# An encoder trunk's FFN: the second projection by seven block products, in three parts of the hidden columns

## The chip, the cores and the metric

The kernel runs on one core of one Trainium2 chip, as one program. Five engines each work through an instruction queue of their own, in order: TensorE (PE; its weight loads are shown as PEld), VectorE (DVE), ScalarE (ACT), GpSimd (POOL) and SyncE (SP, which here issues DMA transfers). They wait for each other by semaphores. Matmuls write into PSUM, of which this kernel has eight banks of 128 x 512 float32. The metric is the device time of one execution in microseconds.

## The reference

A trunk of two layers over 512 tokens of width 1024, all in float32. A layer has a SwiGLU FFN, a mixer (dilated window attention and a convolution branch) and a second FFN. Only the FFNs change:

```python
def swiglu_ffn(h, w_up, w_down):
    a, b = jnp.split(h @ w_up, 2, axis=-1)
    return (jax.nn.silu(a) * b) @ w_down

for l in range(DEPTH):
    x = x + 0.5 * swiglu_ffn(rmsnorm(x, ffn1_norm[l]), ffn1_w_up[l], ffn1_w_down[l])
    x = x + mixer(rmsnorm(x, mix_norm[l]), ...)
    x = x + 0.5 * swiglu_ffn(rmsnorm(x, ffn2_norm[l]), ffn2_w_up[l], ffn2_w_down[l])
    x = rmsnorm(x, final_norm[l])
```

`w_up` is 1024 x 5632, `w_down` 2816 x 1024. So there are four FFNs, each with a hidden width of 2816.

## The kernel before

Activations lie transposed in SBUF: a tile holds 128 features (the partitions) by 512 tokens. The residual x is eight such tiles, `xs[0]` to `xs[7]`. To keep float32 accuracy every operand is split into two parts in a rounded format (float32r): hi, a rounded copy that ScalarE makes, and lo, what is left, which VectorE makes by a subtraction (`split_to`, `stage`). A product is then three matmuls into the same PSUM bank, hi x hi, hi x lo and lo x hi (`mm3`, L157 to L159). The weights are the stationary operand, 128 x 128, and the 512 tokens stream past.

Weights come from DRAM in pieces of up to 1024 columns. `stage` (L151 to L153) transfers one into `raw` (two buffers, issued by SyncE), ScalarE makes `hi` and VectorE `lo` (four buffers each). `proj_cols` walks over such pieces for one or two output tiles.

An FFN has two halves. In the first, for each pair of the 22 hidden tiles, 96 matmuls compute the a and b columns into two banks each (`ps_a` from the three banks of tag `mm`, `ps_b` from the four of tag `at`); VectorE multiplies a by the norm's factors R (L248), ScalarE applies silu (L249), VectorE multiplies by b (L250), and the result is split into a hidden hi and lo tile. All 22 hidden tiles stay in SBUF (44 buffers of tag `h`). The second half, the second projection, goes over the output tiles in groups (0,1), (2,3), (4,5), 6, 7. A group sums over all 22 hidden tiles in its banks (`ps_d`), then VectorE multiplies by 0.5 R (L259) and adds to x (L260), and `after` prepares what the next block needs: the tile times the next norm's gain, split (`xgh`, L174; `xgl`, L175), and a running sum of squares (`sq`, L184 on ScalarE, L188 on VectorE).

Nobody wrote the order of the instructions by hand. A scheduler places each instruction on its engine's queue from the program's order, priorities (`tc.high_priority` moves weight pieces forward) and its own estimates of times; the queues are then fixed, and each engine runs its queue in order. A tile buffer is reused in a ring: who writes into it next waits until its last reader is done.

## Time and profile before

| | us |
|---|---|
| three runs | 2667.84, 2670.09, 2670.85; median 2670.09 |
| the profiled execution | 2669.43, of which its span 2667.5 |
| TensorE busy in the span | 2617.8 (98%), 12125 matmuls |
| VectorE / ScalarE busy | 1599.7 (60%) / 1005.8 (38%) |
| the four second projections | 119.68, 119.68, 119.68, 119.81 |

The span runs from the first instruction to the last. The profile names a group of instructions by line, engine, operation and tiles, as out<-in; `128x512` is partitions by elements. Matmul durations overlap in the pipeline, so the pace of a stage is its length over its matmuls, not the mean duration. "Idle before" is the time that an engine stood still ahead of an instruction, with the engine and tile that released it.

### The profile page before, as it was taken

How to read it: one execution, taken by the hardware profiler on the slowest of the kernel's cores; microseconds unless marked ns; L12 is line 12 of the kernel's file. 1: busy time of each engine (PE TensorE's matmuls, PEld its weight loads, DVE VectorE, ACT ScalarE, POOL GpSimd, SP SyncE). 2: the span in 40 equal slices, each digit the busy share in tenths (PEclk: the TensorE clock that was granted, in tenths of full speed). 3: DMA queues.
4: the chain of work that ended last, by engine and by line, in shares of the span. 5: the costliest groups of instructions: out<-in, count | busy, mean ns of one | idle time of the engine just before them, and what ended most of it. 6: DMA issues, size and time to landing. Idle time of an engine off the chain costs nothing.

```text
span 2667.5 us, 30985 instructions
## 1 busy us (share of the span) xinstructions
PE 2617.8 (98%) x12125; PEld 2125.9 (80%) x12125; DVE 1599.7 (60%) x2606; ACT 1005.8 (38%) x1572; POOL 110.5 (4%) x208
## 2 busy tenths in 40 slices
PE   8999999998999999999999999999989999999998
PEld 6888888776877788888888888887767778888887
DVE  4444349999985754443454433599999756444432
ACT  5332232233578242232332322322344963322222
POOL 1000000011011000000000000000011110000000
PEclk9999999999999999999999999999989999999999
DMA  4332333233333333332333322323323343333322
GB/s 155 98 95 91 103 99 105 79 113 97 100 112 110 117 95 96 102 95 95 95 95 95 100 94 93 108 91 114 96 85 121 100 126 103 95 95 96 102 91 75
DMA packets 253778, 268.65 MB, mean 101 GB/s; under 512 B 11624, under 2 KB 238320, under 8 KB 253632
## 3 DMA queue, kind: packets, MB, share of 16 engines
q1 hardware_dynamic: 242112, 234.91, 28.3%
q0 software_dynamic: 11504, 31.76, 4.0%
q8 instruction: 95, 1.56, 0.2%
q14 instruction: 51, 0.42, 0.1%
q10 hardware_dynamic: 16, 0.00, 0.0%
HBM read 251.75 MB, written 14.88 MB: 100 GB/s over the span
## 4 chain that ended last, share of the span: by engine, by line
PE 88%; DVE 7%; ACT 3%; issue 1%; DMA 0%; SPq 0%; ACTq 0%
PE ps_a L158 6%; PE ps_a L159 6%; PE ps_b L157 6%; PE ps_d L157 6%; PE ps_b L158 6%; PE ps_b L159 6%; PE ps_d L159 6%; PE ps_d L158 6%; PE ps_a L157 6%; PE ps_n L158 4%; PE ps_n L157 4%; PE ps_n L159 3%; DVE cv L516 2%; PE ps_cp L158 1%; PE ps_cp L159 1%; PE ps_cp L157 1%
## 5 line engine op out<-in xcount | busy, mean ns | idle before, releaser
L153 DVE TENSOR_TENSOR lo<-raw,hi 128x1024 fp32r<-128x1024 f32 (+1 forms) x448 | 539.2, 1204 | 725.0 <-ACT hi L152 724.0
L152 ACT ACTIVATE hi<-raw 128x1024 fp32r<-128x1024 f32 (+1 forms) x448 | 468.1, 1045 | 1058.3 <-issue 360.2
L516 DVE SCALAR_TENSOR_TENSOR cv<-u,cwc,cv 128x500 f32<-128x500 f32 (+14 forms) x480 | 335.7, 737 | 0.1
L158 PE MATMUL ps_b<-xgl,hi 128*128 128x512 f32 x704 | 275.1, 391 | 0.0
L157 PE MATMUL ps_a<-xgh,hi 128*128 128x512 f32 x704 | 273.5, 389 | 1.1 <-ACT xgh L174 1.1
L159 PE MATMUL ps_a<-xgh,lo 128*128 128x512 f32 x704 | 274.5, 390 | 0.0
L158 PE MATMUL ps_a<-xgl,hi 128*128 128x512 f32 x704 | 274.3, 390 | 0.1
L157 PE MATMUL ps_b<-xgh,hi 128*128 128x512 f32 x704 | 274.0, 389 | 0.0
L159 PE MATMUL ps_b<-xgh,lo 128*128 128x512 f32 x704 | 273.9, 389 | 0.0
L159 PE MATMUL ps_d<-sh,lo 128*128 128x512 f32 x704 | 273.9, 389 | 0.0
L157 PE MATMUL ps_d<-sh,hi 128*128 128x512 f32 x704 | 273.9, 389 | 0.0
L158 PE MATMUL ps_d<-sl,hi 128*128 128x512 f32 x704 | 273.9, 389 | 0.0
L158 PE MATMUL ps_n<-lo,xgh 128*128 128x512 f32 x576 | 228.7, 397 | 3.9 <-DVE lo L153 3.8
L159 PE MATMUL ps_n<-hi,xgl 128*128 128x512 f32 x576 | 225.7, 392 | 0.0
L157 PE MATMUL ps_n<-hi,xgh 128*128 128x512 f32 x576 | 215.8, 395 | 4.7 <-DVE tmp L379 3.4
L157 PEld LDWEIGHTS ps_a<-xgh,hi 128*128 128x128 f32 x704 | 132.0, 188 | 29.0 <-ACT xgh L174 1.5
L158 PEld LDWEIGHTS ps_b<-xgl,hi 128*128 128x128 f32 x704 | 132.2, 188 | 28.0 <-issue 0.7
L159 PEld LDWEIGHTS ps_b<-xgh,lo 128*128 128x128 f32 x704 | 132.2, 188 | 28.0 <-issue 0.7
L158 PEld LDWEIGHTS ps_a<-xgl,hi 128*128 128x128 f32 x704 | 132.2, 188 | 27.9 <-DVE xgl L175 0.5
L159 PEld LDWEIGHTS ps_d<-sh,lo 128*128 128x128 f32 x704 | 132.2, 188 | 27.5
L159 PEld LDWEIGHTS ps_a<-xgh,lo 128*128 128x128 f32 x704 | 132.2, 188 | 27.5 <-issue 0.2
L157 PEld LDWEIGHTS ps_b<-xgh,hi 128*128 128x128 f32 x704 | 132.2, 188 | 27.4
(234 smaller groups left out, 3988.1 us busy)
## 6 DMA issues: line engine op xcount, KB each, us to landing
raw<-in_ffn_w_up_dram SPq DMA_DIRECT2D x176, 512.0 KB, 3.5
raw<-in_w_in_dram SPq DMA_DIRECT2D x88, 512.0 KB, 3.6
raw<-in_ffn_w_down_dram SPq DMA_DIRECT2D x76, 512.0 KB, 3.5
raw<-in_w_in_dram SPq DMA_DIRECT2D x96, 256.0 KB, 3.1
raw<-in_w_conv_proj_dram SPq DMA_DIRECT2D x16, 512.0 KB, 3.5
raw<-in_w_out_dram SPq DMA_DIRECT2D x16, 512.0 KB, 3.5
vd<-tmp POOLq DMA_DIRECT2D x24, 256.0 KB, 2.3
od<-ot POOLq DMA_DIRECT2D x24, 256.0 KB, 3.0
```

Source lines behind the costliest of these rows:

```text
L152: nc.scalar.activation(hi[:, :m], raw[:, :m], AF.Copy)
L153: nc.vector.tensor_sub(lo[:, :m], raw[:, :m], hi[:, :m].bitcast(F32))
L157: nc.tensor.matmul(ps, ah, bh, start=first, stop=False)
L158: nc.tensor.matmul(ps, ah, bl, start=False, stop=False)
L159: nc.tensor.matmul(ps, al, bh, start=False, stop=last)
L516: nc.vector.scalar_tensor_tensor(a[:, t0:t1], u[k][:, t0 + d:t1 + d], cw(l, j, k), a[:, t0:t1], op0=ALU.mult, op1=ALU.add)
```

## The change

The second projection is computed by the seven-product scheme for 2 x 2 blocks. One block product has two hidden tiles (256 rows of `w_down`), two output tiles, and the tokens in two halves of 256. Directly that is 2 x 2 x 2 = 8 products of 128 x 128 weights by 256 tokens; here it is 7, of which four use sums of weight blocks and four use sums of hidden blocks. `stage7` transfers a weight piece (four hidden tiles by two output tiles), has VectorE form four sums (L251 to L253, tile `sm`) and splits both the raw piece and the sums into hi and lo (`split_to`, L166 and L167). `sums7` does the same for a pair of hidden tiles (tile `ts`, split into `Th` and `Tl`). `proj7` runs the seven products, each three matmuls of 256 columns, into four banks, two products side by side in three of them: the four `at` banks in even groups, the three `mm` banks and the `st` bank in odd ones. When a group is complete, ScalarE copies the first bank (`s1`, L298) and VectorE recombines the banks (L299 to L302, tile `o7`).

The FFN runs in three parts of 8, 8 and 6 hidden tiles: the first projection for these, then the second projection from these alone, added to x (`take`, L338 and L339; the second output tile of a pair comes out with the opposite sign). Hidden tiles and their sums have room for one part. In the last part, output tiles 6 and 7 are computed directly, and `after` runs there only. In all pairs of hidden tiles but the first, the b columns come before the a columns.

The queues change with it. On VectorE, in the second projection of the first FFN (`t<-ps_d` and `x` are the additions into x, `lo` a weight piece); waits name the engine waited for, and DMAHW a transfer. Before:

```order
L153 TENSOR_TENSOR lo_350_2300<-raw_348_2298,hi_349_2299 128x1024 [waits DMAHW1_49,PE_49,Activation_49]
L153 TENSOR_TENSOR lo_353_2330<-raw_351_2328,hi_352_2329 128x512 [waits DMAHW2_49,PE_49,Activation_49]
L153 TENSOR_TENSOR lo_365_2369<-raw_363_2367,hi_364_2368 128x1024 [waits DMAHW3_49,PE_49,Activation_49]
L153 TENSOR_TENSOR lo_368_2399<-raw_366_2397,hi_367_2398 128x1024 [waits DMAHW4_49,PE_49,Activation_49]
L153 TENSOR_TENSOR lo_371_2429<-raw_369_2427,hi_370_2428 128x768 [waits DMAHW5_49,PE_49,Activation_49]
L259 SCALAR_TENSOR_TENSOR t_354_2346<-ps_d_334_2176,R_34_240 128x512 [waits PE_49]
L260 TENSOR_TENSOR x4_85<-x4_85,t_354_2346 128x512 [waits DVE_49]
L259 SCALAR_TENSOR_TENSOR t_358_2356<-ps_d_335_2177,R_34_240 128x512 [waits PE_49]
L153 TENSOR_TENSOR lo_379_2464<-raw_377_2462,hi_378_2463 128x1024 [waits DMAHW6_49,Activation_49]
L260 TENSOR_TENSOR x5_86<-x5_86,t_358_2356 128x512 [waits DVE_49]
```

Now, at the end of the first part's second projection:

```order
L338 SCALAR_TENSOR_TENSOR t_163_1084<-o7_160_1074,R_34_240 128x512
L299 TENSOR_TENSOR o7_180_1203<-ps_7_165_1088,s1_181_1204 128x2x256 [waits PE_49]
L252 TENSOR_TENSOR sm_195_1277<-sm_195_1277,raw_194_1276 128x256 [waits DVE_49]
L339 TENSOR_TENSOR x2_83<-x2_83,t_162_1081 128x512 [waits DVE_49]
L167 TENSOR_TENSOR lo_197_1283<-raw_194_1276,hi_196_1282 128x1024 [waits PE_49,Activation_49]
L339 TENSOR_TENSOR x3_84<-x3_84,t_163_1084 128x512 [waits DVE_49]
L300 TENSOR_TENSOR o7_180_1203<-ps_7_166_1089,o7_180_1203 128x512 [waits DVE_49]
L253 TENSOR_TENSOR sm_195_1277<-sm_195_1277,raw_194_1276 128x256 [waits DVE_49]
L301 TENSOR_TENSOR o7_180_1203<-ps_7_166_1089,o7_180_1203 128x256 [waits DVE_49]
L302 TENSOR_TENSOR o7_180_1203<-ps_7_167_1090,o7_180_1203 128x512 [waits DVE_49,PE_49]
L338 SCALAR_TENSOR_TENSOR t_182_1210<-o7_180_1203,R_34_240 128x512 [waits DVE_49]
L167 TENSOR_TENSOR lo_199_1287<-sm_195_1277,hi_198_1286 128x1024 [waits Activation_49]
```

Pieces that TensorE needs (`lo`), the sums they are made from (`sm`), the recombination (`o7`) and the additions into x stand mixed in one queue, and there is a weight piece every sixth row or so where there was one in two.

On ScalarE, at the same two places, before:

```order
L152 ACTIVATE hi_349_2299<-raw_348_2298 128x1024 [waits DMAHW1_49,PE_49,Activation_49]
L152 ACTIVATE hi_352_2329<-raw_351_2328 128x512 [waits DMAHW2_49,PE_49,Activation_49]
L152 ACTIVATE hi_364_2368<-raw_363_2367 128x1024 [waits DMAHW3_49,PE_49,Activation_49]
L152 ACTIVATE hi_367_2398<-raw_366_2397 128x1024 [waits DMAHW4_49,PE_49,Activation_49]
L152 ACTIVATE hi_370_2428<-raw_369_2427 128x768 [waits DMAHW5_49,DVE_49,PE_49]
L152 ACTIVATE hi_378_2463<-raw_377_2462 128x1024 [waits DMAHW6_49,DVE_49,PE_49]
```

and now:

```order
L166 ACTIVATE hi_176_1153<-raw_174_1147 128x1024 [waits DMAHW2_49,DVE_49,PE_49]
L298 ACTIVATE s1_181_1204<-ps_7_164_1087 128x256 [waits PE_49]
L166 ACTIVATE hi_178_1157<-sm_175_1148 128x1024 [waits DVE_49]
L166 ACTIVATE hi_190_1226<-raw_188_1220 128x1024 [waits DMAHW3_49,Activation_49]
L166 ACTIVATE hi_192_1230<-sm_189_1221 128x1024 [waits DVE_49]
L166 ACTIVATE hi_196_1282<-raw_194_1276 128x1024 [waits DMAHW4_49,DVE_49,PE_49]
L298 ACTIVATE s1_201_1333<-ps_7_184_1216 128x256 [waits PE_49]
L166 ACTIVATE hi_198_1286<-sm_195_1277 128x1024 [waits DVE_49]
```

The copies `s1` of a finished group stand between the hi pieces of the groups behind it.

```diff
--- before.py
+++ after.py
@@ -175,12 +175,17 @@
         nc.vector.scalar_tensor_tensor(lo, src, gain, hi.bitcast(F32), op0=ALU.mult, op1=ALU.subtract)
         return hi, lo
 
+    few = set()
+
+    def tmps(pool):
+        return 5 if id(pool) in few else 7
+
     class SumSq:
         def __init__(self, pool):
             self.pool, self.acc = pool, None
 
         def add(self, src, scale=1.0):
-            t = self.pool.tile([P, S], F32, tag="tmp", name=uniq("sq"), bufs=7)
+            t = self.pool.tile([P, S], F32, tag="tmp", name=uniq("sq"), bufs=tmps(self.pool))
             nc.scalar.activation(t, src, AF.Square, scale=scale)
             if self.acc is None:
                 self.acc = t
@@ -202,7 +207,7 @@
 
     def broadcast_psum(rc, pool):
 
-        dg = pool.tile([P, S], F32, tag="tmp", name=uniq("dg"), bufs=7)
+        dg = pool.tile([P, S], F32, tag="tmp", name=uniq("dg"), bufs=tmps(pool))
         for tt in range(TT):
             nc.vector.tensor_scalar_mul(dg[:, tt * P:(tt + 1) * P], ident, rc[:, tt:tt + 1])
         ps = ps_st(uniq("ps_bc"))
@@ -228,37 +233,123 @@
                     mm3(ps[j], wh[:, k, j * P:(j + 1) * P], wl[:, k, j * P:(j + 1) * P], *rhs[kg], kg == 0, kg == nk - 1)
 
 
+
+
+    HT = S // 2
+
+    def stage7(pool, src):
+
+        nk = src.shape[1]
+        q = nk // 2
+        m = nk * 256
+        raw = wp.tile([P, 1024], F32, tag="raw", name=uniq("raw"), bufs=2)
+        sm = pool.tile([P, 1024], F32, tag="sm", name=uniq("sm"), bufs=2)
+        with tc.high_priority(offset=150):
+            nc.sync.dma_start(raw[:, :m].rearrange("p (a n) -> p a n", a=nk), src)
+            rv = raw[:, :m].rearrange("p (q e n) -> p e q n", q=q, e=4)
+            sv = sm[:, :m].rearrange("p (e q n) -> p e q n", q=q, e=4)
+            nc.vector.tensor_add(sv[:, 0:2], rv[:, 0::3], rv[:, 1][:, None].to_broadcast([P, 2, q, P]))
+            nc.vector.tensor_add(sv[:, 2], sv[:, 1], rv[:, 0])
+            nc.vector.tensor_add(sv[:, 3], sv[:, 2], rv[:, 2])
+            f = []
+            for t in (raw, sm):
+                hi = wp.tile([P, 1024], F32R, tag="hi", name=uniq("hi"))
+                lo = wp.tile([P, 1024], F32R, tag="lo", name=uniq("lo"))
+                split_to(hi[:, :m], lo[:, :m], t[:, :m])
+                p = "p (q e n) -> p e q n" if t is raw else "p (e q n) -> p e q n"
+                f.append([x[:, :m].rearrange(p, q=q, e=4) for x in (hi, lo)])
+        (rh, rl), (sh, sl) = f
+        return [(rh[:, 0], rl[:, 0]), (rh[:, 2], rl[:, 2]), (sh[:, 3], sl[:, 3]), (rh[:, 3], rl[:, 3]),
+                (sh[:, 1], sl[:, 1]), (sh[:, 2], sl[:, 2]), (sh[:, 0], sl[:, 0])]
+
+    def sums7(pool, t2, h2, tag, bufs):
+
+        tv = t2.rearrange("p k (h n) -> p (k h) n", h=2)
+        w = pool.tile([P, 4, HT], F32, tag="w4", name=uniq("ts"), bufs=3)
+        nc.vector.tensor_sub(w[:, 0:2], tv[:, 0::3], tv[:, 1:2].to_broadcast([P, 2, HT]))
+        nc.vector.scalar_tensor_tensor(w[:, 2], w[:, 0], -1.0, tv[:, 3], op0=ALU.mult, op1=ALU.subtract)
+        nc.vector.scalar_tensor_tensor(w[:, 3], w[:, 2], -1.0, tv[:, 2], op0=ALU.mult, op1=ALU.subtract)
+        th = pool.tile([P, 4, HT], F32R, tag=tag, name=uniq("Th"), bufs=bufs)
+        tl = pool.tile([P, 4, HT], F32R, tag=tag, name=uniq("Tl"), bufs=bufs)
+        split_to(th, tl, w)
+        hh, hl = (x.rearrange("p k (h n) -> p (k h) n", h=2) for x in h2)
+        return [(hh[:, 0], hl[:, 0]), (hh[:, 2], hl[:, 2]), (hh[:, 3], hl[:, 3]), (th[:, 3], tl[:, 3]),
+                (th[:, 0], tl[:, 0]), (th[:, 2], tl[:, 2]), (th[:, 1], tl[:, 1])]
+
+    def proj7(pool, src, c0, rhs, odd):
+
+        if odd:
+            bk = [ps_mm(uniq("ps_7")) for _ in range(3)] + [ps_st(uniq("ps_7"))]
+        else:
+            bk = [ps_at(uniq("ps_7")) for _ in range(4)]
+        bv = [x.rearrange("p (h n) -> p h n", h=2) for x in bk]
+
+        home = [(0, 0), (1, 0), (3, 0), (3, 1), (2, 0), (1, 1), (2, 1)]
+        nq = len(rhs)
+        for q0 in range(0, nq, 2):
+            n_ = min(2, nq - q0)
+            w = stage7(pool, src[:, 2 * q0:2 * (q0 + n_), c0:c0 + 256])
+            for q in range(n_):
+                for i in (0, 1, 5, 4, 6, 2, 3):
+                    b, h = home[i]
+                    mm3(bv[b][:, h], w[i][0][:, q], w[i][1][:, q], *rhs[q0 + q][i], q0 + q == 0 and h == 0, q0 + q == nq - 1 and (h == 1 or b == 0))
+        o = pool.tile([P, 4, HT], F32, tag="w4", name=uniq("o7"), bufs=3)
+        s1 = pool.tile([P, HT], F32, tag="s1", name=uniq("s1"), bufs=2)
+        nc.scalar.activation(s1, bv[0][:, 0], AF.Copy)
+        nc.vector.tensor_add(o[:, 0::3], bv[1], s1[:, None].to_broadcast([P, 2, HT]))
+        nc.vector.tensor_add(o[:, 1:3], bv[2], o[:, 3:4].to_broadcast([P, 2, HT]))
+        nc.vector.tensor_add(o[:, 3], bv[2][:, 0], o[:, 2])
+        nc.vector.tensor_add(o[:, 1:3], bv[3], o[:, 1:3])
+        return o.rearrange("p (k h) n -> p k (h n)", k=2)
+
+
+
+
+    PARTS = ((0, 8), (8, 16), (16, 22))
+
     def ffn(l, w_up, w_down, xg, R, after, deferred=None):
         wu = w_up[l].rearrange("(k p) n -> p k n", p=P)
         wd = w_down[l].rearrange("(k p) n -> p k n", p=P)
         with tc.tile_pool(name=uniq("ffn"), bufs=4) as fp:
-            h = []
-            for m in range(0, NF, 2):
-                pss = {}
-                for ab in range(2):
-                    pss[ab] = [ps_mm(uniq("ps_a")) if ab == 0 else ps_at(uniq("ps_b")) for _ in range(2)]
-                    for kk in range(0, KD, 4):
-                        wh, wl = stage(wu[:, kk:kk + 4, ab * FF + m * P:ab * FF + m * P + 256])
-                        for j in range(2):
-                            for k in range(4):
-                                kg = kk + k
-                                mm3(pss[ab][j], wh[:, k, j * P:(j + 1) * P], wl[:, k, j * P:(j + 1) * P], *xg[kg], kg == 0, kg == KD - 1)
-                for j in range(2):
-                    t = fp.tile([P, S], F32, tag="tmp", name=uniq("t"), bufs=7)
-                    nc.vector.tensor_mul(t, pss[0][j], R)
-                    nc.scalar.activation(t, t, AF.Silu)
-                    nc.vector.tensor_mul(t, pss[1][j], t)
-                    h.append(split(fp, t, "h", 2 * NF))
-                if m == 0 and deferred is not None:
-                    deferred()
-            for ts in ((0, 1), (2, 3), (4, 5), (6,), (7,)):
-                pss = [(ps_at if ts[0] in (0, 4, 7) else ps_mm)(uniq("ps_d")) for _ in ts]
-                proj_cols(wd, ts[0] * P, h, NF, pss)
-                for k, ps in zip(ts, pss):
-                    t = fp.tile([P, S], F32, tag="tmp", name=uniq("t"), bufs=7)
-                    nc.vector.scalar_tensor_tensor(t, ps, 0.5, R, op0=ALU.mult, op1=ALU.mult)
+            few.add(id(fp))
+            for m0, m1 in PARTS:
+                h, h7 = [], []
+                for m in range(m0, m1, 2):
+                    pss = {}
+                    for ab in ((0, 1) if m == 0 else (1, 0)):
+                        pss[ab] = [ps_mm(uniq("ps_a")) if ab == 0 else ps_at(uniq("ps_b")) for _ in range(2)]
+                        proj_cols(wu, ab * FF + m * P, xg, KD, pss[ab])
+                    t2 = fp.tile([P, 2, S], F32, tag="t2", name=uniq("t2"), bufs=2)
+                    for j in range(2):
+                        t = t2[:, j]
+                        nc.vector.tensor_mul(t, pss[0][j], R)
+                        nc.scalar.activation(t, t, AF.Silu)
+                        nc.vector.tensor_mul(t, pss[1][j], t)
+                    h2 = split_to(*(fp.tile([P, 2, S], F32R, tag="h", name=uniq("h" + x), bufs=8) for x in "hl"), t2)
+                    for j in range(2):
+                        h.append(tuple(x[:, j] for x in h2))
+                    h7.append(sums7(fp, t2, h2, "T", 8))
+                    if m == 0 and deferred is not None:
+                        deferred()
+                last = m1 == NF
+
+                def take(k, src, f):
+                    t = fp.tile([P, S], F32, tag="tmp", name=uniq("t"), bufs=5)
+                    nc.vector.scalar_tensor_tensor(t, src, f, R, op0=ALU.mult, op1=ALU.mult)
                     nc.vector.tensor_add(xs[k], xs[k], t)
-                    after(k, fp)
+                    if last:
+                        after(k, fp)
+
+                wm = wd[:, m0:m1]
+                for i, ts in enumerate(((0, 1), (2, 3), (4, 5), (6,), (7,)) if last else ((0, 1), (2, 3), (4, 5), (6, 7))):
+                    if len(ts) == 2:
+                        o = proj7(fp, wm, ts[0] * P, h7, i % 2 == 1)
+                        for k in range(2):
+                            take(ts[k], o[:, k], (0.5, -0.5)[k])
+                    else:
+                        pss = [ps_mm(uniq("ps_d"))]
+                        proj_cols(wm, ts[0] * P, h, m1 - m0, pss)
+                        take(ts[0], pss[0], 0.5)
 
 
     def mixer(l, xg, R, rr, after):
```

## Rows read from the trace of the kernel before

**Rows 1.** The page: busy time of each engine, and the granted TensorE clock.
```profile
PE 2617.8 (98%) x12125; PEld 2125.9 (80%) x12125; DVE 1599.7 (60%) x2606; ACT 1005.8 (38%) x1572; POOL 110.5 (4%) x208
PEclk9999999999999999999999999999989999999999
```

**Rows 2.** Windows of the four FFNs' second projections, their matmuls alone: start:end, length, busy, clock.
```profile
257.83:377.51 119.68, 119.68 (x528) 1.00 0.30 93
2534.19:2654.00 119.81, 119.81 (x528) 1.00 0.24 75
sum 478.85, PE 478.85; mean PE 119.71
```

**Rows 3.** One group of that stage (busy, mean ns); timeline there (start, duration in us).
```profile
L157 PE MATMUL ps_d<-sh,hi 128*128 128x512 f32 x176 | 68.5, 389 | 0.0
...
300.22 0.39 PE L158 MATMUL ps_d<-sl,hi 128*128 128x512 f32 x1
300.45 0.39 PE L159 MATMUL ps_d<-sh,lo 128*128 128x512 f32 x1
```

**Rows 4.** Weight loads by form; timeline of an attention score's two matmuls.
```profile
L157 PEld LDWEIGHTS ps_d<-sh,hi 128*128 128x128 f32 x704 | 132.2, 188 | 27.3
...
567.14 0.29 PEld L424 LDWEIGHTS ps_S<-qkT 64*128 64x128 f32 x2 [0.17 <-issue]
567.14 0.70 PE L424 MATMUL ps_S<-qkT 64*128 64x256 f32 x2
```

**Rows 5.** Windows, all engines: a second projection, then a stretch of a first.
```profile
257.83:377.51 119.68, 119.68 (x529) 99.13 (x528) 45.77 (x53) 32.58 (x39) 0.00 (x0) 1.00 0.30 93
134.00:246.00 112.00, 112.00 (x496) 92.78 (x495) 46.56 (x52) 33.36 (x41) 0.00 (x0) 1.00 0.31 96
```

**Rows 6.** VectorE by form: busy us, mean ns, idle before.
```profile
L153 DVE TENSOR_TENSOR lo<-raw,hi 128x1024 fp32r<-128x1024 f32 x428 | 523.2, 1223 | 650.3 <-ACT hi L152 649.2
L175 DVE SCALAR_TENSOR_TENSOR xgl<-x,pcol,xgh 128x512 fp32r<-128x512 f32 x32 | 23.7, 747 | 6.3 <-ACT xgh L174 6.3
L260 DVE TENSOR_TENSOR x<-x,t 128x512 f32<-128x512 f32 x32 | 22.1, 689 | 0.7
L259 DVE SCALAR_TENSOR_TENSOR t<-ps_d,R 128x512 f32<-128x512 f32 x32 | 21.9, 686 | 27.7 <-PE ps_d L159 27.7
L353 DVE TENSOR_TENSOR p<-z,tab 128x256 f32<-128x256 f32 x48 | 20.1, 420 | 0.0
L153 DVE TENSOR_TENSOR lo<-raw,hi 128x768 fp32r<-128x768 f32 x8 | 7.7, 959 | 31.9 <-ACT hi L152 31.9
L327 DVE TENSOR_TENSOR tab<-rt,gqk 128x128 f32<-128x128 f32 x12 | 3.4, 283 | 0.0
```

**Rows 7.** ScalarE by form.
```profile
L152 ACT ACTIVATE hi<-raw 128x1024 fp32r<-128x1024 f32 x428 | 453.7, 1060 | 973.4 <-issue 349.1 <-PE ps_d L158 201.0 <-DMA raw<-in_w_in_dram 83.7
L249 ACT ACTIVATE t<-t 128x512 f32<-128x512 f32 x88 | 54.6, 624 | 101.9 <-DVE t L248 101.9
L461 ACT ACTIVATE ot<-ps_pv 128x256 f32<-128x256 f32 x48 | 22.6, 557 | 12.4 <-PE ps_pv L454 12.3
```

**Rows 8.** The page: DMA issues (KB each, us to landing).
```profile
raw<-in_ffn_w_down_dram SPq DMA_DIRECT2D x76, 512.0 KB, 3.5
```

**Rows 9.** Waits in a second projection: us in total, times, longest.
```profile
DVE lo L153 <- ACT hi L152: 67.7, 21, 5.2
ACT hi L152 <- PE ps_d L158: 66.5, 17, 4.8
```

**Rows 10.** The chain that ended last, at the end of the kernel.
```profile
2653.80 0.24 PE ps_d L159
2654.07 0.70 DVE t L259
2654.80 0.70 DVE x L260
2655.52 0.64 ACT sq L184
```

## The prediction

> **What bounds the kernel now.** I read the engine totals first: TensorE is busy 2617.8 of 2667.5 us and its clock row is full almost everywhere [rows 1], so only what shortens TensorE's own stream, or makes it wait, can move the end. Then the windows of the stage that is changed: in each of the four FFNs the second projection is 528 matmuls of 512 columns in 119.68 us, clock share 1.00 (the 2.4 GHz level), with no idle time [rows 2]. That is 0.2267 us each and 478.8 us in all; the 389 ns that the groups give as the duration of one overlaps the next one, as the starts 0.22 to 0.23 us apart show [rows 3]. VectorE is busy 45.77 us in such a stage, 38% [rows 5], and most of its waiting is for ScalarE, which waits for TensorE to give a weight buffer back [rows 9]. So the helpers follow TensorE today. The question is whether they still do when TensorE gets through its columns faster and each weight block costs VectorE three times as much.
>
> **The matmuls.** A stage of four hidden tiles by two output tiles was 24 matmuls of 512 columns; it becomes 7 products x 2 pairs x 3 split terms = 42 of 256. Per FFN the parts have 8, 8 and 6 hidden tiles: 4 x 84 + 4 x 84 + 3 x 63 = 861 narrow matmuls, and 2 x 18 = 36 wide ones for the last two output tiles. No row shows a narrow matmul of this type. From below, it cannot take less than half of a wide one, 0.113, as its columns still stream. From above, it could be held by its own weight load, which is busy 0.188 [rows 4]; the only 256-column matmuls of the trace, two in plain f32, take 0.70 us with their loads, 0.35 each [rows 4], but that type streams slower, so 0.188 is my upper end. I take 0.120: 512 columns at 2.4 GHz are 0.213, the wide pace leaves 0.0134 per matmul beside the columns, and I keep that whole (0.107 + 0.013). It sits near the lower end because the load hides: in the f32 pair the two loads end 0.29 after the first began, so the second began about 0.10 after the first, under 0.120. Then 861 x 0.120 + 36 x 0.2267 = 111.5 us in place of 119.7: **-8.2 us per FFN, -32.8 in all**. (At 0.113: -55.)
>
> The Trainium skill (TensorE: Matmul & The Clock Gate, Back-to-back issue gap) gives columns / 2.4 GHz plus 2.5 ns. For 512 columns that is 0.216, and the trace has 0.2267, so the rest per matmul is larger here; by that rule a narrow one would cost 0.109, and the term would be about -70 us.
>
> **VectorE's queue in the same stretch.** This is what the saving pays for. A stage of 1024 weight columns costs VectorE one lo piece today, 1.22. Afterwards: sums of 512, 256 and 256 (0.69 + 0.42 + 0.42) and two lo pieces (2.45), 3.97 us, beside 42 x 0.120 = 5.04 us of TensorE. Per pair of output tiles come the recombination (0.69 x 3 + 0.42) and four passes of 0.69 to add into x, 5.25 us per two stages; these were once per FFN and are now once per part [rows 6]. So VectorE needs 2 x 3.97 + 5.25 = 13.2 us for TensorE's 10.1. It can work ahead by two stages only (two raw, two sum, four hi/lo buffers), and the last hidden pair of a part has to go through it as well.
>
> Counted in the new program's order, in part one of the first FFN, from the first multiplication that waits for the part's last first-projection result to the last lo piece that the part's matmuls need, VectorE has 58 instructions: 15 of 1024 columns, 28 of 512, 13 additions of 256 and 2 scalar_tensor_tensor of 256 (no row; 0.45, from 747 against 689 at 512): 18.35 + 19.3 + 5.5 + 0.9 = 44.0 us [rows 6]. In the same stretch TensorE has 12 wide, 309 narrow and 4 wide matmuls: 2.7 + 37.1 + 0.9 = 40.7. So TensorE must wait 3.3 us even if VectorE never idles. Part two: 42.6, 1.9 late. Part three: 38 instructions (6 of 1024, 20 of 512, 8 of 256, 4 of 128), 25.7 against 24.8, 0.9 late [rows 6]. Over the twelve parts this floor is 25 us.
>
> VectorE does idle, because the hi and lo buffers are a ring of two stages. I followed the first part's order by hand with these durations and ScalarE's (hi 1.06, silu 0.62, a 256-column copy out of PSUM 0.56 [rows 7]) and 3.5 us for a weight transfer [rows 8], counting from that first multiplication. (a) The second stage of the first group ends with the last hidden pair, whose T pieces exist at 14.5; its matmuls end at 17.9, and only then may ScalarE write the next stage's two hi pieces: TensorE waits 1.8. (b) In the third group ScalarE's copy s1, which waits until that group's first bank is complete, stands ahead of the hi of the group's second stage: bank complete at 31.7, s1 to 32.3, hi to 33.3, TensorE idle from 31.5: 1.8. (c) The same in the fourth group, where the sums also stand behind VectorE's additions into x until 45.9: hi at 47.0, TensorE idle from 44.8: 2.3. (d) Six waits of 0.15 to 0.95 for one hi or lo piece: 2.5. Sum 8.3 us, the floor in it. Part two has 1.4 us less on VectorE: 6.9. Part three followed the same way: 4.8. **+20 us per FFN, +80 in all.**
>
> **The ends of the FFNs.** The additions into x of the third part's groups pile up behind the last lo. Between there and the mixer VectorE has 30 us of work for tiles that TensorE wants one by one after 8.8 us of its own; along the order, with no idle time, TensorE waits 2.6 us there (twice), and 5.5 before the second layer, where each tile has two sums of squares. At the end of the kernel VectorE has 18.2 us (20 passes of 0.69, the last recombination 2.5, two lo pieces of 768, 1.9) where TensorE has 8.8; today the sum of squares follows the last matmul by about 2.7 (t 0.70, x 0.70, sq 0.64, one addition) [rows 6, 10], so the tail grows by 6.7. **+17.5.**
>
> **At nothing:** the first projection. A pair of hidden tiles costs VectorE 11.7 us there against about 9, beside 96 x 0.2267 = 21.8 us of TensorE; even behind the 12 us left over from a part, no lo piece comes late along the order. ScalarE's 2.1 us per stage hide in 5.04. Five more weight transfers per FFN of the same bytes hide behind the two raw buffers, as long as VectorE frees these.
>
> **Sum.** 2669.4 (this execution: 2667.5 of span, 1.9 around it; the median, 2670.1, lies 0.7 above) - 32.8 + 80 + 17.5 = **2734 us**, 2.4% slower. The narrow matmul's price hardly moves it: at 0.113 the first term is 22 us better, and in the parts, which VectorE sets, some 21 us of that come back as waits.
>
> **Rivals.**
> *VectorE never idles (no change, or just slower).* If the handovers (a) to (d) are absorbed, the floor stays: -32.8 + 25 + 17.5 = +10, 2679. For it: the order was made to interleave three groups' matmuls, and I estimated the transfers. Against: four buffers, and copies ahead of pieces in ScalarE's queue.
> *VectorE does not bound (faster).* If these sums overlap so that TensorE keeps its pace in all twelve parts, only matmuls and ends count: 2669.4 - 32.8 + 17.5 = 2654, or 2632 at 0.113. For it: VectorE has 62% idle in the stage [rows 5]. Against: it decides at 40.7 us of VectorE work in the stretch, and the count has 44.0 from durations that hardly vary.
> *The weight load paces the narrow matmul.* Each product has its own weights, so loads go from 528 to 897 per FFN. At 0.188 each: 861 x 0.188 + 8.2 = 170 us, +50 per FFN; VectorE is then hidden in the parts, some 10 us remain at the ends: 2669 + 201 + 10 = 2880. Against: the loads of [rows 4] that follow 0.10 apart.
> The Trainium skill (Perfetto Trace Analysis, Identifying the Most-Contended Engine) tells one to judge TensorE's room by the load's busy share, not the matmul's. By that rule the stage, with its loads at 99.13 of 119.68 us today [rows 5], has little room for 70% more of them, which is this rival; the trace so far speaks against it only with the f32 loads.
>
> **How the numbers follow.** Forecast (2695 to 2790, with the waits between half and nearly twice my count) 0.72; floor 0.12, two thirds of it beyond 0.2%; faster 0.09; load-paced 0.07. Differences under 0.2% cannot be told from no change here. Slower 0.72 + 0.08 + 0.07 = 0.87, same 0.04, faster 0.09. The range leaves out the faster case and the load-paced one, and takes in the floor: 2678 to 2790.
>
> **What would show it.** In the changed profile: 3444 matmuls into ps_7 whose starts lie 0.12 apart where nothing waits (0.188 would show the load-paced rival); idle time before them of some 80 us, ended by hi and lo pieces; VectorE over 85% busy in the parts' stretches, 48 to 50 us long in the first part; x additions trailing by several us at the end. The forecast is wrong if TensorE is still full in the parts, or if VectorE idles there as much as TensorE does.

## The result, and the profile after

The changed kernel takes 2690.75 us (median of 4 runs, 2688.89 to 2694.37) against 2669.39 for the kernel before on the same chip: a ratio of 1.0082, 95% interval 1.0064 to 1.0099. It is slower, as forecast, and inside the range, but by 21 us and not by 65. The profiled execution has a span of 2686.9 us, 19.4 more than before.

The engine totals, the rows for VectorE and the granted clock from the page of the changed kernel answer to [rows 1]:

```profile
PE 2607.6 (97%) x13601; PEld 2173.2 (81%) x13601; DVE 2068.7 (77%) x3394; ACT 1141.7 (42%) x1704; POOL 110.5 (4%) x208
...
DVE  4767788999986655767778586899999866477767
...
PEclk9999999998999999999999999999999999999999
```

TensorE is busy 10 us less and VectorE 469 us more; its slices reach 8 tenths inside the FFNs now, where they were 3 to 5 (slices 0 to 5 are the first FFN, 15 to 25 the second and third). The timeline of TensorE where the first wide matmuls end and the narrow ones begin (start, duration in us):

```profile
105.74 0.39 PE L159 MATMUL ps_a<-xgh,lo 128*128 128x512 f32 x1
105.97 0.28 PE L157 MATMUL ps<-hh,hi 128*128 128x256 f32 x1
106.08 0.28 PE L158 MATMUL ps<-hl,hi 128*128 128x256 f32 x1
106.20 0.28 PE L159 MATMUL ps<-hh,lo 128*128 128x256 f32 x1
106.32 0.28 PE L157 MATMUL ps<-hh,hi 128*128 128x256 f32 x1
```

(The profile calls these banks ps.) The starts lie 0.12 apart, the price that was taken; the shown 0.28 overlaps the next matmul. Now the windows of the narrow matmuls of the first FFN's three parts: length, then busy us and instructions of PE, PEld, DVE, ACT and POOL:

```profile
105.97:147.70 41.73, 38.47 (x309) 37.27 (x308) 38.08 (x56) 17.45 (x21) 0.00 (x0) 1.00 0.24 72
238.37:279.23 40.86, 38.48 (x310) 37.27 (x308) 36.79 (x54) 17.50 (x20) 0.00 (x0) 1.00 0.21 66
347.90:370.86 22.96, 22.43 (x180) 21.66 (x179) 20.74 (x35) 11.38 (x17) 0.00 (x0) 1.00 0.17 55
```

309 x 0.120 = 37.1, so part one waits 4.6 us, part two 3.8, part three 1.4; the prediction had 8.3, 6.9 and 4.8. The weight loads, busy 37.27 of 41.73 us, do not set the pace. What ends TensorE's waits, from the waits of PE (us in total, times, longest):

```profile
PE ps L157 <- ACT hi L166: 21.9, 25, 1.4
...
PE ps L159 <- DVE lo L167: 2.6, 12, 0.5
```

Most of it is one kind of wait that comes back 13 times over the run, each with the next start 1.70 us after the last one. One of them in TensorE's timeline:

```profile
132.86 0.28 PE L159 MATMUL ps<-hh,lo 128*128 128x256 f32 x1
134.56 0.39 PE L157 MATMUL ps<-Th,hi 128*128 128x256 f32 x1 [1.42 <-ACT hi L166]
```

Beside it ScalarE, which makes the hi piece of the sums (sm) only behind the copy s1 out of PSUM:

```profile
133.18 0.38 ACT L298 ACTIVATE s<-ps 128x256 f32<-128x256 f32 x1 [5.06 <-PE ps L159]
133.46 1.05 ACT L166 ACTIVATE hi<-sm 128x1024 fp32r<-128x1024 f32 x1
134.41 1.05 ACT L166 ACTIVATE hi<-raw 128x1024 fp32r<-128x1024 f32 x1
```

and VectorE, where the last of the three sums of that piece (L253, at 132.56) stands behind other groups' work:

```profile
130.82 1.22 DVE L167 TENSOR_TENSOR lo<-raw,hi 128x1024 fp32r<-128x1024 f32 x1
131.96 0.68 DVE L300 TENSOR_TENSOR o<-ps,o 128x512 f32<-128x512 f32 x1
132.56 0.42 DVE L253 TENSOR_TENSOR sm<-sm,raw 128x256 f32<-128x256 f32 x1
132.89 0.42 DVE L252 TENSOR_TENSOR sm<-sm,raw 128x256 f32<-128x256 f32 x1
```

The three timelines together show what happens. The last sum is ready at 132.98, but its hi piece stands behind s1 in ScalarE's queue. ScalarE has been idle for 5.06 us, because s1 waits for TensorE, up to the end of its last matmul before the stall (132.86 + 0.28). So s1 starts at 133.18 and the hi piece 0.28 later. All 13 waits are like this one: the hi piece starts 0.28 behind the start of an s1, and 0.30 to 1.12 us after its sum was ready, so each costs the same 1.58 us beyond the pace, 20.5 in all. Of the 44 copies these 13 are the only ones that a hi piece follows so closely. But s1 is not all of it: with nothing ahead of it, a hi piece starts about 0.09 behind its sum (the runs below show that), on average 0.73 earlier than here. That is an estimate of 9.5 us for the 13. The other 11 would stay, because the sum itself is ready less than a hi piece's 1.05 us before TensorE needs it.

Look at the starts on VectorE and ScalarE too: 130.82 to 131.96 is 1.14 for an instruction that is shown 1.22 long, 131.96 to 132.56 is 0.60 for one shown 0.68, 133.46 to 134.41 is 0.95 for one of 1.05. The next instruction starts before the shown end of the one before. This will matter.

Where the 19.4 us are, from the starts of the matmuls: the FFNs (each from the start of its first matmul to the start of its last, with the gap between the layers) take 1464.8 us in place of 1447.0, the two mixers 1188.0 in place of 1192.3, the tail behind the last second-projection matmul 19.3 in place of 13.5. Of the FFNs' +17.8, matmuls at 0.120 and 0.2267 give -33; what the starts lie further apart than that in the parts, summed per FFN, is 10.6, 9.6, 10.0 and 11.5, +42 in all; the second layer's start has 5.3 more.

### The profile page after: what moved, and what is told of

Its sections match the earlier page's. It is cut to its first block, busy times and chain, and to the rows that moved or that the text cites. A ratio compares the mean times of both kernels' runs of the same rounds, so it can differ in the third digit from the quotient of the medians.

```text
span 2686.9 us, 35092 instructions
## 1 busy us (share of the span) xinstructions
PE 2607.6 (97%) x13601; PEld 2173.2 (81%) x13601; DVE 2068.7 (77%) x3394; ACT 1141.7 (42%) x1704; POOL 110.5 (4%) x208
## 4 chain that ended last, share of the span: by engine, by line
PE 83%; DVE 11%; ACT 3%; issue 2%; DMA 1%; SPq 0%; DVEq 0%; ACTq 0%
PE ps_b L157 6%; PE ps_a L157 6%; PE ps_a L159 6%; PE ps_a L158 6%; PE ps_b L159 6%; PE ps_b L158 6%; PE ps L159 4%; PE ps L157 4%; PE ps L158 4%; PE ps_n L158 3%; PE ps_n L157 3%; PE ps_n L159 3%; DVE cv L607 2%; DVE lo L153 1%; ACT hi L166 1%
## 5 line engine op out<-in xcount | busy, mean ns | idle before, releaser
L153 DVE TENSOR_TENSOR lo<-raw,hi 128x1024 fp32r<-128x1024 f32 x360 | 439.1, 1220 | 313.8 <-ACT hi L152 300.8
L152 ACT ACTIVATE hi<-raw 128x1024 fp32r<-128x1024 f32 x360 | 379.6, 1055 | 676.1 <-PE ps_a L158 152.6
L607 DVE SCALAR_TENSOR_TENSOR cv<-u,cwc,cv 128x497 f32<-128x497 f32 (+14 forms) x480 | 338.8, 748 | 0.0
L157 PE MATMUL ps<-Th,hi 128*128 128x256 f32 x656 | 183.4, 289 | 22.8 <-ACT hi L166 21.9
L158 PE MATMUL ps<-Tl,hi 128*128 128x256 f32 x656 | 181.1, 283 | 0.0
L159 PE MATMUL ps<-Th,lo 128*128 128x256 f32 x656 | 169.7, 284 | 2.1 <-DVE lo L167 2.1
L166 ACT ACTIVATE hi<-raw 128x1024 fp32r<-128x1024 f32 x88 | 88.0, 1000 | 185.1 <-PE ps L158 119.8
```

What stands on the lines that cost most here:

```text
L152: nc.scalar.activation(hi[:, :m], raw[:, :m], AF.Copy)
L153: nc.vector.tensor_sub(lo[:, :m], raw[:, :m], hi[:, :m].bitcast(F32))
L157: nc.tensor.matmul(ps, ah, bh, start=first, stop=False)
L158: nc.tensor.matmul(ps, ah, bl, start=False, stop=False)
L159: nc.tensor.matmul(ps, al, bh, start=False, stop=last)
L166: nc.scalar.activation(hi, src, AF.Copy)
```

## The experiments

Each but pitch, which is one profiled execution, was timed in turn with the kernel before on the same chip (2669.3 to 2669.8). The table has the medians, and from each profile the same three stretches in us.

| kernel | median | FFNs | mixers | tail |
|---|---|---|---|---|
| before | 2669.4 | 1447.0 | 1192.3 | 13.5 |
| changed | 2690.8 | 1464.8 | 1188.0 | 19.3 |
| parts_direct | 2671.2 | 1448.7 | 1194.9 | 13.5 |
| last_direct | 2687.8 | 1465.7 | 1194.2 | 13.5 |
| s1_vector | 2693.2 | 1473.6 | 1184.7 | 19.3 |
| no_sums | 2656.6 | 1430.9 | 1190.4 | 19.2 |
| x_gpsimd | 2700.7 | 1475.0 | 1191.1 | 19.4 |
| sums_gpsimd | 2682.3 | 1455.5 | 1190.5 | 19.8 |
| x_gpsimd_last | 2692.3 | 1469.2 | 1193.0 | 13.5 |
| gp_last | 2688.4 | 1468.3 | 1189.8 | 13.5 |
| raw_first | 2677.0 | 1442.0 | 1196.6 | 20.6 |
| raw_first_last | 2656.8 | 1441.9 | 1184.9 | 13.5 |
| extra_work | 2696.8 | 1460.6 | 1197.6 | 22.2 |

The mixers' matmuls are the same in all of them, but the scheduler places them in another order in each kernel, and the mixers' length varies from 1184.7 to 1197.6. TensorE's idle time in them varies from 26.2 to 36.6 us, and its time at the lower granted clock (0.50) from 23.9 to 44.4 us; together these explain part of the scatter, and the rest stays open. So a difference of some 10 us between two kernels is read from the FFNs' column.

**parts_direct**: the three parts, with the eight direct products in all of them.

```diff
-                    h7.append(sums7(fp, t2, h2, "T", 8))
...
-                    if len(ts) == 2:
+                    if False:
```

> The FFN in three parts, but with the eight direct block products of before in each (matmuls of 512 columns, no sums, no recombination). It parts the cost of the three parts from that of the seven products. If the parts alone cost nothing (64 more additions into x per kernel of each kind lie beside TensorE): 2668 to 2672. Rival P, in which the parts themselves bring waits (hidden tiles for one part only, a PSUM handover at each of eight more changes between the projections): 2680 to 2690, and then the seven products would nearly pay for themselves.

Measured 2671.18, ratio 1.0005 (0.9996 to 1.0015). Splitting the FFN into parts costs nothing that can be told; the other 20 us belong to the seven products.

**last_direct**: the direct products in the third part alone.

```diff
-                    h7.append(sums7(fp, t2, h2, "T", 8))
+                    if m1 != NF:
+                        h7.append(sums7(fp, t2, h2, "T", 8))
...
-                    if len(ts) == 2:
+                    if len(ts) == 2 and not last:
```

> Seven products in the first two parts only; the third part's second projection is direct, so that no recombination and no sums stand behind the last weight pieces of an FFN. Matmuls cost 1.8 us more per FFN (7.2). The trace of the changed kernel has 1.8 us of waits per FFN in the third part, 5.3 at the start of the second layer and some 6 to 7 at the end of the kernel, together some 19: expected 2690.7 + 7 - 19 = 2679. If the ends don't come from VectorE's backlog: 2690 to 2698.

Measured 2687.79, ratio 1.0066 (1.0051 to 1.0081): between the 2679 of the one theory and the 2690 of its rival. The ends go as the first says (tail 13.5, the second layer's start as before), but that buys back matmuls (189 narrow at 0.120 become 108 wide at 0.2267, about 1.8 us per FFN), the two remaining parts wait as much as three did (9.5 to 13.0 us per FFN; three stretches of 3.4 us at the lower clock are in it), and the mixers lose what they had gained.

**s1_vector**: the copy s1 goes from ScalarE to VectorE, so that no hi piece stands behind it.

```diff
-        nc.scalar.activation(s1, bv[0][:, 0], AF.Copy)
+        nc.vector.tensor_copy(s1, bv[0][:, 0])
```

> The copy s1 of a finished group's first bank runs on VectorE in place of ScalarE; all else as in the changed kernel. Theory Q (queue order): in the changed kernel TensorE waits in the parts mostly because s1, which waits for its bank, stands ahead of the hi pieces in ScalarE's queue; the thirteen waits of about 1.5 us go (20 us), so 2669 to 2676. Theory V (VectorE's amount of work): VectorE sets the pace of the parts, and 44 copies of about 0.33 us more on it make them longer: 2695 to 2705.

Measured 2693.20, ratio 1.0082 (1.0065 to 1.0099). Neither theory has its range: ScalarE's queue had 2669 to 2676, and the time is just under the 2695 of the other. With the copy gone the hi pieces wait for the sums, and each starts some 0.09 behind its last sum. ScalarE's timeline of this kernel:

```profile
134.66 1.06 ACT L166 ACTIVATE hi<-sm 128x1024 fp32r<-128x1024 f32 x1 [5.20 <-DVE sm L253]
135.62 1.04 ACT L166 ACTIVATE hi<-raw 128x1024 fp32r<-128x1024 f32 x1
137.19 1.06 ACT L166 ACTIVATE hi<-sm 128x1024 fp32r<-128x1024 f32 x1 [0.53 <-DVE sm L253]
```

This does not show that s1 was harmless on ScalarE, because the run changes two things. It takes the copy from ahead of the hi pieces, and it puts 44 x 0.33 = 14.5 us onto VectorE, which makes the sums. The 8.8 us more in the FFNs can be what is left of a gain on one engine and a loss on the other. No run moves s1 within ScalarE's queue alone, so its own share stays the estimate of 9.5 us from the changed kernel's trace.

**no_sums**: leaves the three weight sums out of each stage; the second split takes the raw weights again.

```diff
-            nc.vector.tensor_add(sv[:, 0:2], rv[:, 0::3], ...)
-            nc.vector.tensor_add(sv[:, 2], sv[:, 1], rv[:, 0])
-            nc.vector.tensor_add(sv[:, 3], sv[:, 2], rv[:, 2])
...
-            for t in (raw, sm):
+            for t in (raw, raw):
```

> Leaves out the three VectorE additions that form the sums of weight blocks (L251 to L253); the second split takes the raw piece again. 76 full and 12 half stages lose about 1.2 us of VectorE each, and the hi piece no longer waits for VectorE. Theory V: VectorE drops well under TensorE in the parts, all 42 us of waits there go, 2645 to 2652. Theory Q: the waits behind s1 (20 us) stay, the others partly go: 2668 to 2680.

Measured 2656.61, ratio 0.9947 (0.9927 to 0.9967): 4.6 above the one theory's range, 11 below the other's. The starts in the parts lie only 1.3 to 2.5 us per FFN behind the pace. TensorE itself can do the narrow matmuls at 0.120 all through; without the sums on VectorE it hardly waits. This run does not part late sums from s1 either: its hi pieces wait for no sums, and on ScalarE's queue they stand elsewhere. The instruction behind an s1 starts 0.43 or more after it in all 44 cases, never 0.28. This leaves two readings: VectorE has too much to do there (amount), or the hi pieces of the sums come too late although it has the time (order).

**x_gpsimd, sums_gpsimd, x_gpsimd_last, gp_last** take work off VectorE, to GpSimd: the additions into x of the first two parts, the weight sums, the former with the third part direct, and all three.

```diff
-                    nc.vector.tensor_add(xs[k], xs[k], t)
+                    (nc.vector if last else nc.gpsimd).tensor_add(xs[k], xs[k], t)
...
-            nc.vector.tensor_add(sv[:, 0:2], rv[:, 0::3], ...)
+            nc.gpsimd.tensor_add(sv[:, 0:2], rv[:, 0::3], ...)
```

> The additions into x of the first two parts (16 per FFN) go from VectorE to GpSimd, nothing else changes. On VectorE one starts the next independent instruction 0.60 us later, so about 9.6 us of VectorE's queue per FFN go, those that stand just ahead of the recombination's additions and the weight sums of the next group. Theory V (the waits of about 10 us per FFN are weight sums that come late in VectorE's queue): the waits of the two first parts (about 8.5 us per FFN) fall by a third to two thirds, 2668 to 2680. Rival Q2 (the weight sums are late because each depends on the one before it, not because of what stands ahead): 2687 to 2692, the waits as they are. Rival G (GpSimd's additions are slow, or slow VectorE's down while both work): slower than 2692, and VectorE's instructions longer in the trace than 0.69 us for 512 elements.

> The three weight sums of each stage go from VectorE to GpSimd. Without them altogether 2656.6 was measured, with waits in the parts of 1.3 to 2.5 us per FFN. Theory V: if GpSimd makes the three sums of a stage (512, 256 and 256 elements) in less than the 2.9 us that a stage of narrow matmuls lasts (24 times 0.12), 2657 to 2668, and the kernel beats the one before (2669.4). Rival G: GpSimd takes longer than 2.9 us a stage, or takes VectorE's time while it works; then TensorE waits for each stage: 20 stages per FFN by 1 to 3 us each, 2750 and above.

> As x_gpsimd, and the third part takes the direct products (the ends of the FFN as before the change). Alone, the direct third part was worth 3 us (2687.8). Theory V: the waits left in the two parts fall by a third to two thirds of 9 to 10 us per FFN: 2662 to 2677. Q2: 2686 to 2690. Rival G: above 2690.

> The weight sums and the additions into x on GpSimd, the third part direct. Theory V: the waits in the two parts nearly go, the ends are those of before; 112.3 minus 107 us of matmuls per FFN is what is left as a gain: 2648 to 2660. Rival G, the sums on GpSimd taking longer than 2.9 us a stage: 2730 and above.

Measured 2700.74 (ratio 1.0118, 1.0103 to 1.0133), 2682.27 (1.0048, 1.0033 to 1.0063), 2692.29 (1.0087, 1.0072 to 1.0102) and 2688.44 (1.0070, 1.0053 to 1.0086). Only the sums alone gain, 8 us, and far less than the 2657 to 2668 of the theory. The rival of a slow GpSimd that slows VectorE is right in kind and in time for the two x_gpsimd runs, but its 2750 and 2730 for the other two are far off. Those rested on 2.9 us per stage (24 matmuls); a stage has 42, 5.04 us, and GpSimd's three sums take 1.54 + 1.31 + 1.11 = 3.95 us on average. From x_gpsimd, first GpSimd's timeline, then VectorE's beside it:

```profile
130.76 3.76 POOL L339 TENSOR_TENSOR x<-x,t 128x512 f32<-128x512 f32 x2 [114.52 <-DVE t L338]
```

```profile
131.05 2.32 DVE L167 TENSOR_TENSOR lo<-raw,hi 128x1024 fp32r<-128x1024 f32 x1
133.29 0.68 DVE L300 TENSOR_TENSOR o<-ps,o 128x512 f32<-128x512 f32 x1
133.89 0.90 DVE L253 TENSOR_TENSOR sm<-sm,raw 128x256 f32<-128x256 f32 x1
134.72 0.41 DVE L252 TENSOR_TENSOR sm<-sm,raw 128x256 f32<-128x256 f32 x1
```

GpSimd takes some 1.9 us for a 512-column addition. While it works, VectorE's lo piece of 1.22 takes 2.32, a sum of 0.42 takes 0.90, and an addition with an input from PSUM keeps its 0.68; when GpSimd is done, 0.41 is back. So part of what is moved is paid for on VectorE. The Trainium skill (Perfetto Trace Analysis, Optimizing Scalar/DVE Operations) says that the two share a read port into SBUF and that moving work between them might not help; these rows agree. These four runs say nothing on amount against order.

**raw_first** leaves VectorE's work and moves TensorE's need: in each stage the products that need no sums come first.

```diff
-        home = [(0, 0), (1, 0), (3, 0), (3, 1), (2, 0), (1, 1), (2, 1)]
+        home = [(0, 0), (1, 0), (3, 1), (3, 0), (2, 0), (1, 1), (2, 1)]
...
-            for q in range(n_):
-                for i in (0, 1, 5, 4, 6, 2, 3):
+            for i, q in [(i, q) for ii in ((0, 1, 3), (5, 4, 6, 2)) for q in range(n_) for i in ii]:
...
-        nc.vector.tensor_add(o[:, 1:3], bv[3], o[:, 1:3])
+        nc.vector.tensor_add(o[:, 1], bv[3][:, 1], o[:, 1])
+        nc.vector.tensor_add(o[:, 2], bv[3][:, 0], o[:, 2])
```

> Within each stage the narrow matmuls of the three products that need no weight sums come first, for both pairs of the stage; those of the four products with sums follow (the third half-bank and the fourth change places, so that each bank still begins with its first half). The first matmul that needs a sum comes 18 narrow matmuls after the stage's first in place of 6: 12 times 0.12 = 1.44 us later. The instructions of VectorE and ScalarE are those of the changed kernel (one 512-element addition becomes two of 256, 0.06 us more on VectorE per block). Theory H (handover: the sums are ready about 1.5 us late at the head of a group, and VectorE has time left): the 13 waits of 1.5 us (20 us) and most of the shorter ones go, 2655 to 2672; up to 42 us of waits in the parts are there to win. Rival A (amount: VectorE has no time left in the parts, as the prediction's floor had it): a wait that is pushed back comes again later in the same part, 2683 to 2691.

In the source's order a group's first bank is also complete 12 matmuls earlier, so that s1 can go earlier. Measured 2676.95, ratio 1.0027 (1.0017 to 1.0037), 14 us less than the changed kernel. Its waits of TensorE in the parts:

```profile
PE ps L157 <- ACT hi L166: 7.7, 8, 1.0
...
PE ps L159 <- DVE lo L167: 3.3, 12, 0.3
```

The starts in the parts lie 4.3 us per FFN behind the pace in place of about 10, and the FFNs are 23 us shorter, 5 below those of the kernel before. So most of it was the order: the same work on VectorE, and TensorE waits less than half as long. But rival A is not quite out. Eight waits are left, one near the end of the first and of the second part of each FFN, with starts 1.24 apart. One of them, with ScalarE and VectorE beside it, and the engines' busy time in this part from 120.40 on:

```profile
144.93 0.38 PE L157 MATMUL ps<-Th,hi 128*128 128x256 f32 x1 [0.96 <-ACT hi L166]
...
143.29 0.38 ACT L297 ACTIVATE s<-ps 128x256 f32<-128x256 f32 x1 [6.06 <-PE ps L159]
143.81 1.06 ACT L166 ACTIVATE hi<-sm 128x1024 fp32r<-128x1024 f32 x1
...
143.30 0.42 DVE L253 TENSOR_TENSOR sm<-sm,raw 128x256 f32<-128x256 f32 x1
...
120.40:149.36 28.96, 27.65 (x220) 26.53 (x219) 28.96 (x47) 10.96 (x13) 0.00 (x0) 1.00 0.23 74
```

In all eight the hi piece starts 0.09 to 0.10 behind its sum and 0.5 behind s1, so here it is the sum that is late; and VectorE has had no idle time since 120.40 (28.96 of 28.96 us). What is left looks like amount, which extra_work tests. The run does not tell how much of the gain came from the sums' later need and how much from the earlier s1. The total misses 2655 to 2672 because this kernel has the longer mixers and the longer tail of the table.

**raw_first_last** is the same with the third part direct.

> As raw_first, with the third part by the eight direct products. Alone, the direct third part took 2.9 us off the changed kernel, with 9 to 13 us of waits per FFN in the two remaining parts. Theory H: those waits go too, 2645 to 2665, faster than the kernel before by 0.2 to 0.9%. Rival A: 2680 to 2688.

Measured 2656.82 (2655.74 to 2657.18), ratio 0.9951 (0.9937 to 0.9964): 0.5% faster than the kernel before, the best version here. Of its 13 us, 5 lie in the FFNs; 7 lie in the mixers, where TensorE is idle for 26.2 us in place of 31.9; I would not count on that part.

**pitch** measures VectorE by itself: the kernel before, with three chains of additions behind its last ones.

```diff
+            for i in range(64):
+                nc.vector.tensor_add(xs[i % 8], xs[i % 8], xs[i % 8])
+            for i in range(64):
+                nc.vector.tensor_add(xs[0], xs[0], xs[1])
+            for i in range(64):
+                k = xs[i % 8][:, (i // 8 % 2) * 256:(i // 8 % 2) * 256 + 256]
+                nc.vector.tensor_add(k, k, k)
```

> The kernel before with 192 additions on VectorE behind its last ones: 64 of 512 elements, each on a tile of its own in turn (independent of the one before), 64 of 512 elements, each on the result of the one before, and 64 independent of 256 elements. Theory: independent ones start 0.60 us (512) and 0.33 us (256) apart although each is shown 0.69 and 0.42 us long, and dependent ones 0.73 us apart, so the stretches last 38, 47 and 21 us. Rival (the shown duration is what an instruction takes of VectorE's queue, as the prediction reckoned): 44, 44 to 47 and 27 us.

VectorE's timeline there (2771.07 us in all; rows with a count are runs of like instructions, the duration that of the run; the short row is part of the 256-column chain):

```profile
2663.85 36.80 DVE L709 TENSOR_TENSOR x<-x 128x512 f32<-128x512 f32 x61
...
2714.45 0.68 DVE L711 TENSOR_TENSOR x<-x,x 128x512 f32<-128x512 f32 x1
2715.05 4.10 DVE L714 TENSOR_TENSOR x<-x 128x256 f32<-128x256 f32 x12
...
2719.08 43.55 DVE L711 TENSOR_TENSOR x<-x,x 128x512 f32<-128x512 f32 x60
```

Independent 512-column additions start (36.80 - 0.68) / 60 = 0.602 us apart though each is shown 0.68 long; dependent ones (43.55 - 0.68) / 59 = 0.727; independent 256-column ones (4.10 - 0.42) / 11 = 0.335. The theory's three numbers hold, and the shown duration is not what an instruction takes of the queue. The Trainium skill (Perfetto Trace Analysis, Optimizing Scalar/DVE Operations) says the same: a profiled instruction shows about twice the access overhead, since its second half overlaps the next instruction.

**extra_work** asks how much room VectorE has left in raw_first: one more 512-column addition per block.

```diff
+        ex = pool.tile([P, 2, HT], F32, tag="ex", name=uniq("ex"), bufs=1)
+        nc.vector.tensor_add(ex, o[:, 0:2], o[:, 2:4])
```

> As raw_first, with one more addition of 512 elements on VectorE behind each block's recombination (its result goes nowhere): 11 per FFN, 44 in all, 0.60 us each by the starts. In raw_first VectorE stands idle for 2.4 us of the 43.6 us of part one of the first FFN, all of it before 120.4, and then has no idle time up to the end of the part. Theory S (room left: the work that TensorE waits for is done in time, and only the additions into x fall further behind, into the first projection's VectorE idle time): 2677 to 2684. Rival A (amount: VectorE's queue is at its limit in the parts, and what is added comes back as waits of TensorE in full): 44 times 0.60 = 26 us more, 2698 to 2706.

Measured 2696.79, ratio 1.0108 (1.0091 to 1.0125): 20 us for 26 us of VectorE's time, 1.2 below the range of rival A and far above that of theory S. The waits of PE:

```profile
PE ps L159 <- DVE lo L167: 22.4, 24, 2.1
```

Now it is the lo pieces, VectorE's own, that come late, 22.4 us in place of 3.3. So raw_first stands at the edge of VectorE's amount: 4.3 us of waits per FFN without the additions, and most of the full price with them. (About 6 us of the 20 are some 65 narrow matmuls that run 0.21 apart behind such waits, 0.09 more than 0.12; the granted clock there is 0.53 to 0.59.)

## Why the prediction was right in sign and wrong in size

**The matmuls held**: 0.120 for a narrow one, -33 us. The load-paced rival is out; loads of 0.188 hide under a matmul every 0.12.

**The step that failed is "VectorE's queue in the same stretch"**, whose +80 measured 42. It summed the durations of the groups [rows 6] as if the next instruction began at the shown end. The forecast did make that correction for TensorE (389 ns shown, 0.2267 apart [rows 3]) and not for VectorE, though VectorE's timeline of the kernel before shows it too:

```profile
558.03 0.73 DVE L516 SCALAR_TENSOR_TENSOR cv<-u,cwc,cv 128x500 f32<-128x500 f32 x1
558.68 0.42 DVE L352 TENSOR_TENSOR p<-z,tab 128x256 f32<-128x256 f32 x1
559.01 0.42 DVE L353 TENSOR_TENSOR p<-z,tab 128x256 f32<-128x256 f32 x1
```

0.42 shown, 0.33 to the next. At 0.08 to 0.09 us per independent instruction, 58 of them are up to 5 us. The trace of the changed kernel has the same 58 instructions, from 103.45 to 148.21 (the count takes in the start of one more):

```profile
103.45:148.21 44.76, 39.97 (x59) 1.00 0.27 83
```

So 44.0 was 40.0 with overlaps counted once, against TensorE's 40.7. VectorE is over 85% busy in part one, as forecast (38.08 of 41.73), but the part is not 48 to 50 us long. The floor of 25 us over twelve parts was not there. The prediction's own sign of being wrong, that VectorE idles in the parts as much as TensorE does, came true: by the windows above VectorE is idle 3.65, 4.07 and 2.22 us in the three parts, TensorE 3.26, 2.38 and 0.53. It is a matter of 2 us per part, which is why it decides: raw_first nearly fits, extra_work does not.

**The handovers** were counted at 55 us beside the floor (80 - 25) and about 42 came. (b) and (c), a hi of the sums held by s1, are what the trace shows: 13 times 1.58 us, 20.5 in all, against 1.8 and 2.3 each in eight parts. The mechanism of (b) was right, and its size nearly. What (b) left out is that the sum behind s1 is late too, as (c) has it: by the estimate above s1's place in the queue is some 9.5 us of the 20.5, and no run shows that share by itself. Wait (a), on the ring of buffers, did not come.

**The ends**: the tail grew by 5.8 (6.7 forecast) and the second layer's start by 5.3 (5.5), of which two waits in TensorE's timeline of the changed kernel:

```profile
1340.55 0.50 PE L158 MATMUL ps_a<-xgl,hi 128*128 128x512 f32 x1 [1.27 <-DVE xgl L175]
...
1352.22 0.50 PE L157 MATMUL ps_a<-xgh,hi 128*128 128x512 f32 x1 [1.16 <-ACT xgh L174]
```

Both go with a direct third part (last_direct). Of the 2.6 us in front of each mixer 0.9 and 1.3 came, by the starts of TensorE's matmuls; the first of these waits is

```profile
390.72 0.50 PE L157 MATMUL ps_gg<-xgh,hi 128*128 128x512 f32 x1 [0.70 <-ACT hi L152]
```

Before the change and in last_direct there are none. The mixers still came out 4.3 shorter as a whole, in the scatter that is only partly explained.

**"At nothing"**: parts_direct confirms it for the split itself, within its interval of -0.04 to +0.15%.

**Sum by its own terms, as measured**: -33 + 42 + 5.3 + 5.8 - 4.3 = +16, and some 3.5 us more spread over the FFNs, +19.4. Of the rivals, "VectorE never idles" came nearest in time, 2679, with a mechanism that fell: there was no floor, and what came were waits for late pieces. The time fell into the forecast's range only because that took in this rival's 2679; it does not speak for the floor. What should have warned: the floor was the small difference of two large counts, 44.0 and 40.7, and only one of them had been reckoned from start to start.

## What to carry to other kernels

To ask whether an engine can keep up, count start to start in a stretch where it never idles, and never add up shown durations: on VectorE that was 13% off for 512 columns, and it turned a fit into a floor. Where a scheme adds sums to the operands, let the products that need no sums go first in each stage; that took 23 us off these FFNs without less work on any engine. In an in-order queue look for an instruction that waits for the very engine that needs the next one: s1 waited for TensorE's bank while TensorE waited for the hi piece behind it. When one engine is at its limit, test it by giving it more work as well as less; and when a test moves an instruction, ask what it costs where it goes (s1_vector).

## What was not expected of the hardware

- VectorE's next independent instruction starts about 0.08 us before the shown end of the one before (0.602 for 0.68, 0.335 for 0.42); a dependent one starts 0.04 behind it.
- GpSimd's additions slow VectorE's while they run (2.32 in place of 1.22 in x_gpsimd), but not the one there that reads PSUM (0.68 as ever).
- The clock can fall within a part. In x_gpsimd TensorE waits 1.66 us after shorter waits, and its windows then read (length, PE busy, granted clock, DMA share, GB/s):

```profile
134.00:136.00 2.00, 0.34 (x4) 1.00 0.10 5
136.00:138.00 2.00, 2.00 (x10) 0.52 0.81 257
138.00:139.40 1.40, 1.40 (x8) 0.50 0.00 0
139.40:141.00 1.60, 1.60 (x15) 0.97 0.00 0
```

At the lower level, 1.2 GHz, the narrow matmuls are 0.21 apart. After the changed kernel's wait of 1.42, before 134.56, the clock stayed at 1.00; in last_direct it fell after a wait of the same 1.42 us, so the length of one wait does not tell:

```profile
267.90 0.39 PE L157 MATMUL ps<-Th,hi 128*128 128x256 f32 x1 [1.42 <-ACT hi L166]
...
269.80:273.20 3.40, 3.40 (x16) 0.50 0.28 76
```
